# Parking the gating results in DRAM and re-spacing five stages of a one-core decoder step

## The chip, the cores and the metric

The kernel runs on one core of one Trainium2 chip. The metric is the device time of one execution in microseconds (us). Three runs of the kernel before took 2204.79, 2202.24 and 2200.46 us, so its median is 2202.24 us. Its engines are named PE (TensorE), DVE (VectorE), ACT (ScalarE), POOL (GpSimd) and SP (SyncE, which issues nearly all DMAs).

## The reference

One layer of a decoder trunk over 1024 prompt tokens and 32 sample tokens (8 requests of 4), with model width 1024. Reduced to what the kernel's stages compute:

```python
h = layer_norm(ALPHA * x + 0.5 * swiglu(x, f1_w1, f1_w3, f1_w2))      # FFN A, LN1
z = h @ w_in + b_in                                                   # q, k, v | u, v | gates ga, gb
# attention: 3 groups of 4 heads, (window, dilation) = (128,1), (512,4), (2048,16), T5 bias
att = sum over groups of o_g * softmax_g(logsumexp_g)                 # combine_groups
# spatial gating
z = gelu(uv); u, vr = z[..., :512], z[..., 512:]
vn = layer_norm(vr, ln_g, ln_b)
yb = u * (tril(ws) @ vn + sb)                                         # in chunks of 128 tokens, 4 groups of 128
mix = (sigmoid(ga) * (att @ w_oa) + sigmoid(gb) * (yb @ w_ob)) @ w_out
h = layer_norm(ALPHA * h + mix)                                       # LN2
h = layer_norm(ALPHA * h + 0.5 * swiglu(h, f2_w1, f2_w3, f2_w2))      # FFN B, LN3
```

where `swiglu(x, w1, w3, w2) = (silu(x @ w1) * (x @ w3)) @ w2` with a hidden width of 2816.

## The kernel before, in words

Activations lie transposed: features on the 128 partitions, the 1056 tokens as columns, in four chunks `c` of 264. Every float32 operand of a product is split into a rounded half `hi` and a remainder `lo` (`split`: a cast on ACT, a subtraction on DVE), and a product is three matmuls, hi x hi, hi x lo and lo x hi (`mm3`, L227). All weights come in units of 128 x 1024 or smaller (`unit`: a load into a raw tile, then a split).

In order of time, the stages are: FFN A's hidden blocks by a Strassen scheme (to about 467 us); the down product w2, most of it in nine rounds of seven products (467 to 657), then four plain blocks in dense form, one output block after the other, their evictions at L885; LN1, chunk by chunk (`start_ln`, `norm`); six gate blocks; the other products of z in pairs; ten more gate blocks ("tail gates", to about 1240) beside which the attention and the spatial gating run; w_ob; w_oa; w_out with LN2; FFN B in the same way as A; LN3.

The work beside the products is written as generators. After each product block, `tick` lets the queues `bg`, `slow` and `mid` make a few steps each, so the attention (`attend`, six times: two pairs of heads by three groups), the gating (`sgu_norm`, then four `sgu_mix`) and the norms come between products. One attention step computes scores (L1164), a masked minimum on DVE (L1172), exponentials on ACT (L1176), transposes on PE (L1187) copied back by L1191, and the products with the values (L1203). After each attention its maxima and sums (`ml`) are transposed (L1225) and stored to the DRAM tensor `mlD`; after three attentions a combine reads them back, computes the softmax over the groups (L1261 to L1274), stores the factors to `cD` (L1276) and loads them spread over the partitions (L1283), by which the attention outputs are multiplied (L1288 to L1291). The scheduler orders instructions on each engine by recorded order and priority; `high_priority` and `urgent` move something ahead, `issue_after` holds something behind.

Lines that the later steps touch: `sgu_norm` normalises v over tokens, with a square root on ACT (`rsqrt`, L630) and nine normalisations (L1447). `sgu_mix` writes its split result into two tiles `yb[gg]` that stay in SBUF until w_ob. `mix` multiplies each product of w_ob or w_oa into its gate (L1505). `units2` makes the w2 units for the dense blocks, of which the last come while the dense blocks run. `column_sums`, `centers` subtract the column means for LN1 (L537). `copy_state` appends state copies `ws<-st`, which no one waits for, to weight loads. The pool of 128 x 1056 tiles has 37 slots (`S`), that of weight halves 8 (`W`).

Of the kernel before, what the change touches and what calls it, by code (L numbers as in the profile page):

```python
# [13 lines left out]
F32R = mybir.dt.float32r  # L14
AF = mybir.ActivationFunctionType
# [5 lines left out]
P = 128  # L21
# [39 lines left out]
LATE = 16  # L61
# [3 lines left out]
WARM = 2  # L65
FENCED = (mybir.EngineType.DVE, mybir.EngineType.Activation, mybir.EngineType.SP)
# [5 lines left out]
EARLY = 6  # L72
# [7 lines left out]
class Trunk:  # L80
# [131 lines left out]
    def unit(self, src, n=D, slot=False, ahead=URGENT):  # L212
        new = self.S if slot else self.W
        with self.tc.high_priority(offset=ahead):
            raw = self.R([P, D])
# [3 lines left out]
        self.fence[mybir.EngineType.SP] = dma.ins  # L219
        self.copy_state(dma, 1)  # L220
        return hi, lo
# [133 lines left out]
    def prep(self, src, f, H, engine):  # L355
# [7 lines left out]
        self.copy_state(dma, 2)  # L363
# [154 lines left out]
    def center(self, c, hs, rest, m=None, parts=1):  # L518
# [15 lines left out]
        for j in range(2):  # L534
# [3 lines left out]
            yield  # L538
# [43 lines left out]
    def norm(self, c, i, mode, Y, s):  # L582
# [7 lines left out]
        r, t = self.X([P, 3], "rs"), self.X([P, 3], "rt")  # L590
        self.rsqrt(r, t, pv, EPL)
# [35 lines left out]

    def rsqrt(self, r, t, v, eps):
# [12 lines left out]
    def ffn(self, w13, w2p, w2, i, mode, resid):  # L641
        nc, preps = self.nc, {}
        last = FB + NG * (KB // 2) - 1
# [27 lines left out]
        else:  # L671
# [3 lines left out]
            self.step(self.bg, 1)  # L675
            begin(1)
            for c in range(NC):
                self.drain(lns.pop(c))
                self.hidden8(units, 0, c)
                if c:  # L680
                    with self.chained():
                        next(preps[1], None)
            self.bg.append(s1)
# [5 lines left out]
        def ready(f):  # L689
            for _ in preps.pop(f):  # L690
                pass
            if f < last:
                begin(f + 1)

        def between(f, bg, slow=0):
            if f + 1 in preps:
                next(preps[f + 1], None)
# [8 lines left out]
        for f in range(1, FB):  # L706
# [5 lines left out]
            def after():  # L712
# [4 lines left out]
            self.hidden(f, after)  # L717
# [67 lines left out]
    def out(self, w2, i, mode, ready, between, load):  # L785
        nc = self.nc
        f = FB
        self.w2units, self.spare = self.units2(w2), False
# [4 lines left out]
        def fetch(k):  # L793

            if k < NPL:
                H.append(self.load_hidden(k))

# [33 lines left out]
        for g in range(NG):  # L831
            for np in range(KB // 2):
                final = g == NG - 1 and np == KB // 2 - 1
                if g == NG - 2 and np == 0:
                    self.bg.append(sums)
                if g == 0 and np == 1 and mode != "out":
# [7 lines left out]
                ready(f)  # L844

                def step(p):
# [6 lines left out]
                    if final:  # L853
                        fetch(k + 1)
                        if k in (4, 6):
                            W2.append(next(self.w2units))
# [16 lines left out]
        self.spare = True  # L873
# [13 lines left out]
        for c in range(NC):  # L887
            early = 6 if c == 0 else 0
            if mode != "out":
                self.hold_normed(c)  # L890
                if c == 2:
                    self.early = [self.unit(self.a["wzp"][n], slot=True, ahead=AFTER) for n in range(CHUNKED)]
            for n in range(KB):
# [4 lines left out]
                if c == 0 and n in (1, 3):  # L898
                    W2.append(next(self.w2units))
# [147 lines left out]
    def widen(self):  # L1047
# [6 lines left out]
        self.jD = self.dp.tile([6, 64, 66], F32, name="jD")  # L1054
        self.zD = [self.dp.tile([P, NT], F32, name=f"zD{n}") for n in range(42)]
# [21 lines left out]
        for n in range(CHUNKED, NLEAD):  # L1077
            w = self.unit(a["wzp"][n])
            if n == NLEAD - 1:
                begin(0)  # L1080
            for c in (1, 3, 0, 2):
                self.gate8(w, DENSE[n], c, AF.Sigmoid, STEPS["lead"], 1)
                if n == NLEAD - 1:
                    next(preps[0], None)
# [33 lines left out]
    def attend(self, i):  # L1118
# [19 lines left out]
        self.fetch_qkv(i + 1)  # L1138
# [77 lines left out]
        for t in range(6):  # L1216
# [4 lines left out]
            if t < 4:  # L1221
                scores(t)
            yield from self.pause(SPREAD)
# [12 lines left out]
    def combine(self, hp):  # L1236
# [3 lines left out]
        for g in range(3):  # L1240
            x = raw[:, g]
            for m in range(2):
                for h in range(2):
                    src = self.mlD[hp, g, m, h]
                    o = x[8 * h : 8 * h + 8, m]
                    if g == 0:
                        nc.sync.dma_start(o, src.rearrange("(a x) -> a x", a=8))
                    elif g == 1:
                        nc.sync.dma_start(
                            o.rearrange("p (r b) -> p r b", r=4), src.rearrange("(r a b) -> a r b", r=4, a=8)  # L1250
# [543 lines left out]
```

## Time and profile before

| What | Value |
|---|---|
| Median of three runs | 2202.24 us (2200.46 to 2204.79) |
| The profiled execution | 2200.98 us |
| Its span | 2199.2 us |
| Mean granted TensorE clock | 0.988 |
| Instructions | 43234 |
| PE, DVE, ACT, POOL busy | 97%, 71%, 41%, 15% |
| DMA moved | 429.82 MB, mean 195 GB/s |

The profile gives one execution. Its time is 1.8 us longer than its span, since the span begins with the first instruction recorded. In a row of a group, "x" gives the number of instructions, then come busy time and mean ns of one, then the idle time of that engine just before them and the operation that ended most of it. "A <- B" in a row of waits reads: A waited for B. A granted clock of 1.00 is full speed.

### The profile page before, as it was taken

The numbers are of one execution on the slowest core, as the hardware profiler recorded it, in microseconds if no ns is written. First come the engines' busy times: TensorE is split into PE (matmuls) and PEld (weight loads), VectorE is DVE, ScalarE is ACT, GpSimd is POOL, SyncE is SP. The second block draws the span as 40 slices with busy tenths as digits, with TensorE's granted clock in tenths as the row PEclk, the third lists the DMA queues.
The fourth block names the chain that finished last, engine by engine and source line by source line (L and its number), as shares of the span: only waits on it lengthen the run. The fifth ranks groups of instructions, "written<-read, shape, count | busy, mean of one in ns | idle before, by whom it ended". The sixth has DMA issues, their size and how long they took to land.

```text
span 2199.2 us, 43234 instructions
## 1 busy us (share of the span) xinstructions
PE 2133.2 (97%) x17281; PEld 2092.9 (95%) x17281; DVE 1564.8 (71%) x2718; ACT 898.1 (41%) x1690; POOL 330.1 (15%) x238
## 2 busy tenths in 40 slices
PE   9999999999998999999989998998999999999997
PEld 8999999999998999999879897998999999999997
DVE  8777776656788725887674648778676776657787
ACT  5444444421225634344465354246444444322224
POOL 0432332200010022232000000000432332100000
PEclk9999999999999999999989999999999999999999
DMA  4435545598873325666854547513445545596751
GB/s 157 146 134 177 179 161 177 193 367 324 330 279 136 135 102 188 215 215 221 313 165 152 172 156 245 187 51 126 165 158 178 171 161 185 186 384 264 295 192 79
DMA packets 170553, 429.82 MB, mean 195 GB/s; under 512 B 24864, under 2 KB 61456, under 8 KB 167664
## 3 DMA queue, kind: packets, MB, share of 16 engines
q1 hardware_dynamic: 169920, 426.53, 55.3%
q8 instruction: 135, 2.21, 0.4%
q10 hardware_dynamic: 432, 0.54, 0.1%
q14 instruction: 66, 0.54, 0.1%
HBM read 305.97 MB, written 167.22 MB: 215 GB/s over the span
## 4 chain that ended last, share of the span: by engine, by line
PE 81%; DMA 7%; DVE 7%; ACT 2%; issue 1%; POOL 1%; SPq 1%; ACTq 0%; DVEq 0%; POOLq 0%
PE ax L227 43%; PE mm L227 35%; DMA M<-kv 4%; DVE W L239 1%; PE ax L1164 1%; DMA zD<-M 1%; DMA S<-zD 1%; PE ax L1203 1%; DVE S L239 1%; PE ax L1187 1%; DMA R<-wz 0%; DVE X L1346 0%; DVE S L608 0%; DVE X L1361 0%; DVE M L1345 0%
## 5 line engine op out<-in xcount | busy, mean ns | idle before, releaser
L227 PE MATMUL ax<-S,W 128*128 128x264 f32 x5472 | 716.2, 284 | 0.8 <-ACT S L994 0.5
L227 PE MATMUL mm<-S,W 128*128 128x264 f32 x5040 | 677.4, 289 | 25.8 <-DVE S L1505 9.3
L227 PEld LDWEIGHTS ax<-S,W 128*128 128x128 f32 x5472 | 685.6, 188 | 3.3 <-ACT S L994 1.5
L227 PEld LDWEIGHTS mm<-S,W 128*128 128x128 f32 x5040 | 641.6, 191 | 43.1 <-issue 10.7
L227 PE MATMUL ax<-S,S 128*128 128x264 f32 x3288 | 483.7, 285 | 2.9 <-DVE S L1003 2.8
L227 PEld LDWEIGHTS ax<-S,S 128*128 128x128 f32 x3288 | 434.2, 188 | 4.1 <-DVE S L1003 4.1
L227 PE MATMUL mm<-S,S 128*128 128x264 f32 x2496 | 388.4, 286 | 9.0 <-ACT S L238 4.0
L227 PEld LDWEIGHTS mm<-S,S 128*128 128x128 f32 x2496 | 337.7, 189 | 11.5 <-ACT S L238 4.4
L238 ACT CAST W<-R 128x256 fp32r<-128x256 f32 (+2 forms) x172 | 127.6, 759 | 316.8 <-PE mm L227 118.2
L369 POOL TENSOR_TENSOR Q<-R 128x512 f32<-128x512 f32 x50 | 72.1, 1443 | 793.1 <-DMA R<-w13b 217.1
L239 DVE TENSOR_TENSOR W<-R,W 128x256 fp32r<-128x256 f32 (+2 forms) x172 | 152.6, 891 | 28.2 <-ACT W L238 24.0
L238 ACT CAST W<-Q 128x1024 fp32r<-128x1024 f32 (+1 forms) x79 | 77.9, 986 | 217.1 <-POOL Q L370 91.7
L780 DVE SCALAR_TENSOR_TENSOR S<-ax,S 128x264 f32<-128x264 f32 x240 | 99.9, 431 | 69.6 <-PE ax L227 68.5
L444 DVE TENSOR_TENSOR S<-ax,M 128x264 f32<-128x264 f32 x84 | 33.7, 433 | 150.6 <-PE ax L227 150.6
L106 POOL CAST S<-ones 128x1 fp32r<-128x1 f32 x32 | 18.3, 594 | 745.5 <-PE mm L227 663.8
L239 DVE TENSOR_TENSOR S<-Q,S 128x1024 fp32r<-128x1024 f32 (+1 forms) x79 | 111.8, 1415 | 3.5 <-ACT S L238 3.3
L239 DVE TENSOR_TENSOR W<-Q,W 128x1024 fp32r<-128x1024 f32 (+1 forms) x79 | 92.0, 1164 | 24.5 <-ACT W L238 24.5
L238 ACT CAST S<-Q 128x1024 fp32r<-128x1024 f32 (+1 forms) x79 | 77.8, 985 | 74.1 <-PE ax L227 55.0
L238 ACT CAST S<-R 128x512 fp32r<-128x512 f32 (+1 forms) x65 | 44.6, 686 | 116.5 <-DMA sumsA<-S 42.6
L239 DVE TENSOR_TENSOR S<-S,M 128x528 fp32r<-128x528 f32 x72 | 85.6, 1189 | 2.1 <-ACT M L238 0.2
L370 POOL TENSOR_TENSOR Q<-Q,R 128x512 f32<-128x512 f32 x50 | 83.6, 1673 | 2.7
L377 POOL TENSOR_TENSOR Q<-R,Q 128x512 f32<-128x512 f32 x50 | 82.7, 1653 | 1.2
(199 smaller groups left out, 2063.3 us busy)
## 6 DMA issues: line engine op xcount, KB each, us to landing
ws<-st SPq DMA_DIRECT2D x144, 256.0 KB
S<-sumsA SPq DMA_DIRECT2D x63, 528.0 KB
S<-sumsB SPq DMA_DIRECT2D x63, 528.0 KB
M<-kv SPq DMA_DIRECT2D x96, 256.0 KB
sumsA<-M SPq DMA_DIRECT2D x90, 264.0 KB
sumsB<-M SPq DMA_DIRECT2D x90, 264.0 KB
R<-w13b SPq DMA_DIRECT2D x44, 512.0 KB
S<-zD SPq DMA_DIRECT2D x42, 528.0 KB
```

Of the source, the lines that this page charges most:

```text
L106: self.nc.gpsimd.tensor_copy(t[:, 0, :1] if len(shape) == 3 else t[:, :1], self.ones[:, :1])
L227: mm = lambda a, b, s, e: nc.tensor.matmul(o, a[:, cc], b, start=s, stop=e, skip_group_check=True)
L238: a = self.nc.scalar.copy(hi, src)
L239: b = self.nc.vector.tensor_tensor(lo, src, hi.bitcast(F32), op=ALU.subtract)
L369: tt(s12[:, lo], cd[:, lo], cd[:, hi], op=ALU.add)
L370: tt(s12[:, hi], s12[:, lo], ab[:, lo], op=ALU.subtract)
L377: tt(s34[:, hi], ab[:, hi], s12[:, hi], op=ALU.subtract)
L444: go(one, 5, False, lambda x: tt(h[:, x, 1], one[x], p7[:, x], op=ALU.add))
L780: nc.vector.scalar_tensor_tensor(y(x, r, e), bank[x], HALF, y(x, r, e), op0=ALU.mult, op1=ALU.add)
L1164: nc.tensor.matmul(pS[h][:, r, :nk], q[e, i * P : (i + 1) * P], k[e, k0 : k0 + nk], start=True, stop=True)
L1187: nc.tensor.transpose(pT[r][:, h, o], s[:, r, h, o], self.ident)
L1203: nc.tensor.matmul(pv[0][e, (i % 4) * P : (i % 4 + 1) * P], V[:, i - (nb - 1) + b, e], sT[:, r, h, b * P : b * P + P], start=b == 0, stop= ...
```

## The change

All parts are in one file:

- **Gate weights ahead.** `part_gates` loads the six lead gate units while FFN A's seven-product rounds run, splits them, and stores both halves to DRAM (`gates`). `gate_unit` loads the halves, so no split remains at the gate blocks. The rounds carry one state copy fewer for each pair of weight loads, and `units2` none.
- **w2 units.** All four are made in the last seven-product round (`last`, `FINAL`), the centre subtractions of a chunk are spaced.
- **Norms.** `rsqrt_dve` computes an inverse square root on DVE, by an integer estimate and three Newton steps. It replaces the square root on ACT in the last chunk of LN2, in chunk 2 of LN3, and in `sgu_norm`. After LN2's chunk 2, ACT evaluates a Silu once.
- **FFN B's first blocks.** Blocks 0 and 19 are computed densely at the start, where before block 0 alone was; 19 was in the Strassen scheme.
- **Spatial gating.** Its steps are spaced, the sample rows of v are written out by a generator of their own (`sgu_rows`) at the end, and each `sgu_mix` stores its two halves to DRAM (`ybD`); `fetch_yb` loads them in four places during the last tail gates (`load`, `FETCH`), the fourth result after them.
- **Attention loads.** The next attention's q, k, v are loaded at step 3 of the running one instead of its beginning; a combine reads `mlD` in nine loads instead of twelve and loads the factors of its third group later.
- **w_ob.** `EARLY` goes from 6 to 5: blocks 5, 6 and 7 are computed at w_oa's blocks 1, 3 and 5, instead of blocks 6 and 7 at w_oa's blocks 0 and 1. Sigmoids of late gates change place with it, and `LATE` goes from 16 to 6.

The core of the diff:

```diff
+    def part_gates(self, *units):
+        yield from self.pause(4 * MID)
+        for n in units:
+            lo, hi = self.S([P, D]), self.S([P, D], F32R)
+            self.nc.sync.dma_start(lo, self.a["wzp"][n])
+            yield from self.pause(2 * MID)
+            self.split(hi, lo.bitcast(F32R), lo)
+            yield from self.pause(MID)
+            for t, dst in zip((hi.bitcast(F32), lo), self.gates[n]):
+                self.nc.sync.dma_start(dst, t)
+            yield
...
+    def rsqrt_dve(self, r, t, x, v, eps):
+        nc = self.nc
+        tt = nc.vector.scalar_tensor_tensor
+        nc.vector.tensor_scalar(x, v, eps, None, op0=ALU.add)
+        nc.vector.tensor_scalar(r.bitcast(I32), x.bitcast(I32), -0.5, MAGIC, op0=ALU.mult, op1=ALU.add)
+        for _ in range(3):
+            nc.vector.tensor_tensor(t, x, r, op=ALU.mult)
+            tt(t, t, -0.5, r, op0=ALU.mult, op1=ALU.mult)
+            self.chain = tt(r, t, 1.5, r, op0=ALU.add, op1=ALU.mult).ins
...
+            lead = [units] + [[self.unit(w13[f, x]) for x in range(2)] for f in plain[1:]]
             begin(1)
             for c in range(NC):
                 self.drain(lns.pop(c))
-                self.hidden8(units, 0, c)
...
+                for f, u in zip(plain, lead):
+                    self.hidden8(u, f, c)
...
-            yield self.unit(w2[u * n : u * n + n].rearrange("(p x) -> p x", p=P), D, self.spare)
+            yield self.unit(w2[u * n : u * n + n].rearrange("(p x) -> p x", p=P), D, u > 1, raw=self.Q if u > 1 else self.R, copies=0)
...
-                if c == 0 and n in (1, 3):
-                    W2.append(next(self.w2units))
...
-        self.rsqrt(rs[:, 0], rs[:, 1], mv[:, :, 1], EPS)
+        self.rsqrt_dve(rs[:, 0], rs[:, 1], mv[:, :, 1], mv[:, :, 1], EPS)
...
+        yield from self.pause(MID)
+        for t, dst in zip((hi, lo), self.ybD[gg]):
+            nc.sync.dma_start(dst, t.bitcast(F32))
+
+    def fetch_yb(self, gg):
+        t = [self.S([P, NT], F32R) for _ in range(2)]
+        for x, src in zip(t, self.ybD[gg]):
+            self.nc.sync.dma_start(x.bitcast(F32), src)
+        self.yb[gg] = t
...
+        def load(c):
+            while any(g in self.mid for g in sgu[: c + 1]):
+                self.step(self.mid, 1)
+            with self.tc.high_priority(offset=URGENT):
+                for g in FETCH[c][1]:
+                    self.fetch_yb(g)
+                for n in FETCH[c][0]:
+                    mt[n] = self.fetch_z(34 + n)
...
-            if n < KB - EARLY:
-                local(EARLY + n)
+            if n % 2 and EARLY + n // 2 < KB:
+                local(EARLY + n // 2)
```

with `FETCH = ((), ((0,), (0,)), ((1, 2), (1,)), ((3,), (2,)), ((4, 5), (3,)))`: for each chunk, the gates and then the gating results to load; the last entry is for the call after the tail gates.

The order that the scheduler makes of it, at three places. First SP, at the second combine, before: the loads from `mlD` have gone ahead, the factors are stored and spread, and gate loads (`zD`) follow.

```order
L1276 DMA cD<-S_15282 16x128 x3
L1283 DMA S_15315<-cD 64x1024 x2
L1283 DMA S_15316<-cD 64x1024 x2
L1283 DMA S_15317<-cD 64x1024
L1102 DMA S_15434<-zD_8671 128x1056
L1102 DMA S_15511<-zD_8672 128x1056
```

And now, at the same place:

```order
L1289 DMA mlD<-X_15271 32x128
L1304 DMA S_15318<-mlD 16x2x128
L1309 DMA S_15318<-mlD 8x4x32 x4
L1626 DMA Q_15823<-wout 128x1024
L1309 DMA S_15318<-mlD 8x16x8 x4
L1333 DMA cD<-S_15318 16x128 x3
L1343 DMA S_15348<-cD 64x1024 x2
L1343 DMA S_15351<-cD 64x1024 x2
L1343 DMA S_15388<-cD 64x1024
L1562 DMA S_15460<-yb_8666 128x1056
L1562 DMA S_15461<-yb_8667 128x1056
L1160 DMA S_15464<-zD_8706 128x1056
```

The two halves of the fourth gating result (`yb_8666`, `yb_8667`) now stand behind the combine's loads.

Second PE, at the end of the last attention. Before, w_ob products (a tile of w_ob is `W_15583` or `W_15584`, a gating result `S_13534` to `S_13919`) run beside it and go on after the ml transpose (L1225).

```order
L1187 MATMUL ax_15189<-ident,S_15135 128x128 x2
L1187 MATMUL ax_15188<-ident,S_15135 128x128 x2
L1225 MATMUL ax_15235<-ident,X_14981 32x128
L227 MATMUL mm_15631<-S_13765,W_15583 128x264
L227 MATMUL mm_15631<-S_13766,W_15583 128x264
L227 MATMUL mm_15631<-S_13765,W_15584 128x264
L227 MATMUL mm_15631<-S_13918,W_15583 128x264
```

Now, with the third result in `S_15279` and `S_15280` and the fourth in `S_15460` and `S_15461` (products of the same form in between are left out):

```order
L1285 MATMUL ax_15269<-ident,X_15011 32x128
L1261 MATMUL ax_15217<-S_15228,Q_14998 64x128 x4
L253 MATMUL mm_15477<-S_15279,W_15469 128x264
...
L253 MATMUL mm_15517<-S_15280,W_15469 128x264
L253 MATMUL mm_15517<-S_15279,W_15470 128x264
L253 MATMUL mm_15477<-S_15460,W_15469 128x264
```

After the ml transpose (now L1285) come four value products and nine products with the third result, and then products with the fourth. Three tiles (`mm_15477`, `mm_15495`, `mm_15517`) are begun in parallel, since the first three results are used ahead of the fourth.

Third ACT, at the gating's norm. Before:

```order
L630 ACT_TABLE_LOAD
L630 ACTIVATE X_13274<-X_12957,eps_163 128x9
L1145 COPY Q_13366<-ax_13367 128x512
L1210 COPY S_12932<-ax_13231 128x512
L1145 COPY Q_13366<-ax_13373 128x512
L1447 ACTIVATE S_12952<-S_12952,X_13274 128x512 x2
L1447 ACTIVATE S_12953<-S_12953,X_13274 128x512 x2
L1447 ACTIVATE S_12954<-S_12954,X_13274 128x512 x2
L1447 ACTIVATE S_12955<-S_12955,X_13274 128x512 x2
L1447 ACTIVATE S_12956<-S_12956,X_13274 32x512
L1176 ACT_TABLE_LOAD
L1176 ACTIVATE S_13415,X_13413<-S_13415,X_13413 128x128
```

Now (L1009 evicts a gate product, L1234 are the exponentials, L1249 copies transposes):

```order
L1249 COPY S_13447<-ax_13440 128x512
L1249 COPY S_13447<-ax_13439 128x2x128
L1511 ACTIVATE S_12976<-S_12976,X_13468 128x512 x2
L1511 ACTIVATE S_12977<-S_12977,X_13468 128x512 x2
L1511 ACTIVATE S_12978<-S_12978,X_13468 128x512 x2
L1511 ACTIVATE S_12979<-S_12979,X_13468 128x512 x2
L1511 ACTIVATE S_12980<-S_12980,X_13468 32x512
L1009 ACTIVATE M_13714<-mm_13689,cols 128x264
L1234 ACTIVATE S_13450,X_13422<-S_13450,X_13422 128x128
```

The square root and both table loads have gone; the nine normalisations still follow each other.

More of the change, by code (lines that the diff above doesn't have):

```diff
@@ L60 @@
 AFTER = 100
-LATE = 16
+LATE = 6
 MID = 3
@@ L642, in ffn @@
         nc, preps = self.nc, {}
-        last = FB + NG * (KB // 2) - 1
+        plain = PLAIN[: 1 if i == 0 else 2]
+        blocks = [f for f in range(FB) if f not in plain] + [FB + g for g in range(NG * (KB // 2))]
+        after = dict(zip(blocks, blocks[1:]))
         def begin(f):
@@ L704, in load @@
                     loads.popleft()()
-        for f in range(1, FB):
+        for f in blocks[: FB - len(plain)]:
             ready(f)
@@ L1536, in mix @@
         units = self.A = None
-        while any(g in self.mid for g in sgu):
-            self.step(self.mid, 1)
+        load(NC)
         def column_sums():
```

158 lines of the change are left out of this document (98 added, 60 removed).

## The prediction

> **What bounds the kernel now.** I read the page first, then the waits of TensorE by stretch, then the stretches with the largest loss. The page: TensorE is busy nearly all the time and holds four fifths of the chain that ended last.
>
> ```profile
> span 2199.2 us, 43234 instructions
> PE 2133.2 (97%) x17281; PEld 2092.9 (95%) x17281; DVE 1564.8 (71%) x2718; ACT 898.1 (41%) x1690; POOL 330.1 (15%) x238
> PE 81%; DMA 7%; DVE 7%; ACT 2%; issue 1%; POOL 1%; SPq 1%; ACTq 0%; DVEq 0%; POOLq 0%
> ```
>
> The stretches (from:to, length, busy time with number of instructions for PE, weight loads, DVE, ACT, POOL, then granted clock, DMA share, GB/s) give the price of a product and show where TensorE loses.
>
> ```profile
> 50.00:460.00 410.00, 410.00 (x3367) 410.00 (x3366) 293.30 (x400) 175.71 (x311) 121.58 (x76) 1.00 0.51 174
> 1080.00:1345.00 265.00, 244.61 (x1990) 220.60 (x1991) 158.31 (x463) 137.62 (x367) 0.00 (x0) 0.96 0.58 183
> 1120.00:1160.00 40.00, 30.96 (x223) 26.37 (x223) 32.41 (x85) 25.13 (x60) 0.00 (x0) 0.79 0.61 187
> 460.00:660.00 200.00, 199.57 (x1604) 194.92 (x1603) 145.82 (x316) 39.72 (x63) 5.99 (x12) 1.00 0.86 324
> 1342.00:1388.00 46.00, 38.28 (x268) 35.86 (x269) 42.27 (x67) 21.40 (x25) 1.93 (x2) 0.93 0.67 232
> 1480.00:1530.00 50.00, 43.24 (x331) 42.09 (x331) 44.58 (x56) 32.27 (x45) 3.28 (x4) 0.93 0.37 128
> ```
>
> Undisturbed, 410 us hold 3367 products: 0.122 us each. That is TensorE's pace, and a change that leaves the products alone can win only where it idles or is granted a lower clock. The attention stretch 1080:1345 idles for 20.4 us at a clock of 0.96. The waits of TensorE (who waited for whom: us, times, longest) name the causes, in turn for 1060:1400, 655:710 and 1480:1540:
>
> ```profile
> PE ax L1187 <- ACT S L1176: 10.0, 4, 5.9
> PE mm L227 <- DVE S L1505: 9.3, 9, 3.2
> PE mm L227 <- ACT M L954: 5.0, 3, 2.9
> PE mm L227 <- ACT S L238: 2.3, 1, 2.3
> ```
>
> ```profile
> PE mm L227 <- DVE S L885: 3.8, 3, 2.5
> PE mm L227 <- DVE S L239: 2.4, 1, 2.4
> ```
>
> ```profile
> PE mm L227 <- ACT S L238: 4.0, 1, 4.0
> PE mm L227 <- ACT M L415: 2.7, 3, 1.9
> ```
>
> **What the change wins.** *w2 and LN1.* Before, four unit splits of w2 stand in VectorE's queue among the evictions of the dense w2 blocks (L885), next to unbroken centre subtractions.
>
> ```profile
> 672.62 1.22 DVE L239 TENSOR_TENSOR S<-R,S 128x1024 fp32r<-128x1024 f32 x1
> 673.75 2.42 DVE L537 TENSOR_TENSOR S<-S,ax 128x1056 f32<-128x1056 f32 x2
> ```
>
> The change makes all four units in the last seven-product block and spaces the subtractions, so 4 x 1.22 = 4.9 us of VectorE leave this place. The 3.8 + 2.4 = 6.2 us of waits lose their cause: I take -6 (range -7 to -2, if the last loads of that block land late).
>
> *Gating norm.* ScalarE held its queue for a square root with its table load, nine normalisations, and the load back before the attention's exponentials could run:
>
> ```profile
> 1119.93 1.28 ACT L630 ACT_TABLE_LOAD   x1
> ...
> 1124.34 6.46 ACT L1447 ACTIVATE S<-S,X 128x512 f32<-128x512 f32 x9 [0.27 <-DVE X L1443]
> 1130.82 1.28 ACT L1176 ACT_TABLE_LOAD   x1
> ```
>
> Both table loads go (2.56 us). The nine normalisations still stand in one run, but the changed order puts 16 + 59 = 75 products between the scores and transposes on either side of it, 75 x 0.122 = 9.1 us, against 6.46 us and four exponentials. The stretch 1120:1160 shows 9.0 us without TensorE, and its clock of 0.79 costs 31 x 0.21 = 6.5 us more; of these 15.5 I take -12 (-15 to -5). Of the other waits for exponentials (10.0 - 5.9 = 4.1) and of the 5.0 for gate outputs the slower pace of the gating should remove half: -5 (-8 to +2). The new rsqrt is some eleven tiny VectorE instructions in series; the trace has none, so I bound it between 0 and 11 x 0.42 = 4.6 (the row of L1505 below, a far larger operation) and cost it at nothing, because gate products go on beside it.
>
> *w_oa stage.* Here VectorE is the bound: in 1342:1388 it is busy 42.3 of 46 us, while 268 products need 32.7. Two more w_ob blocks come into this stretch. Each brings 48 x 0.122 = 5.9 us of TensorE work, but only four product evictions and a weight split to VectorE (groups of 1312:1322.6: busy, mean ns):
>
> ```profile
> L1505 DVE TENSOR_TENSOR S<-S,mm 128x264 f32<-128x264 f32 x7 | 2.9, 416 | 3.4 <-PE mm L227 3.4
> ...
> L239 DVE TENSOR_TENSOR W<-R,W 128x512 fp32r<-128x512 f32 x1 | 0.7, 671 | 0.0
> ```
>
> 4 x 0.42 + 0.7 = 2.4 us. So 11.7 us of products are done for 4.8 us of VectorE, a win of 6.9 if the interleaving is perfect and 0 if it is not at all: -6 (-8 to -1). Two table loads more (the late gates' sigmoids and the sample softmax now alternate) lie on ScalarE, busy 21.4 of the 46 us.
>
> *FFN B's start.* The 4.0 + 2.7 us of waits go with the table switches around the last LN2 chunk:
>
> ```profile
> 1497.79 1.28 ACT L630 ACT_TABLE_LOAD   x1
> ...
> 1499.37 1.28 ACT L415 ACT_TABLE_LOAD   x1
> ```
>
> With the second plain block some 140 products stand between the last chunk's norm and its first use, where 24 stood. Doing it densely costs 24 products, 2.9 us; the clock (0.93 over 43 us) gives back some 3. Sum -5 (-7 to +1).
>
> The Trainium skill, ScalarE: Activation LUTs, section "What ACT_TABLE_LOAD costs", puts a switch at about 2.66 us, because a drain follows the load. By the rows a switch is 1.28 us; by that page the switches removed here (four of them on the path) would be worth 5.5 us more than their rows, an estimate from the page.
>
> **What the change costs.** Parking the gating results moves 8.5 MB through DRAM. What matters is where the last reload stands. In the changed SyncE order it comes behind the whole second combine: ml to DRAM, nine loads back, VectorE's combine, three stores to cD, five broadcast loads, and only then the two halves of result 3. TensorE's order has the first w_ob products behind attention 5, each needing result 3 for its last quarter; the 27 products of three tiles that do without it are used up earlier. The trace of before shows that same chain, harmless there because the results never left SBUF:
>
> ```profile
> 1309.29 0.27 PE L1225 MATMUL ax<-ident,X 128*32 128x128 f32 x1
> ...
> 1322.60 1.26 SPq L1276 DMA_DIRECT2D cD<-S  x3
> 1324.02 3.04 SPq L1283 DMA_DIRECT2D S<-cD  x5
> ...
> 1329.24 1.23 DVE L1288 TENSOR_TENSOR S<-S,S 128x1024 f32<-128x1024 f32 x1 [1.61 <-DMA S<-cD]
> ```
>
> From the ml transpose to the end of the five issues are 1327.1 - 1309.3 = 17.8 us. Twelve loads become nine (-1 us), and VectorE is not shared with the seven product evictions of the row above (-2.9 us): 14. Then the reload must land: the first broadcast load took 1329.2 - 1324.0 = 5.2 us; the reload (1.08 MB behind 1.3 MB of broadcast data) I put at 7 (5 to 13). That is 21 us after the transpose. Cover: value products and nine w_ob products, some 2 us. So TensorE waits **+19** (+8 if ScalarE and VectorE run ahead, +25), and after such an idle time the clock dips: +2, from 1120:1160, where 0.21 over 10 us is 2.1.
>
> The Trainium skill, TensorE: Matmul & The Clock Gate, Part 1, says that after an idle window of some 3.4 us the clock falls to half and needs as long of work to return; by that, one wait of 19 us costs 1.7 us of clock, an estimate from the page, no more than one of 6 us. The row above, 6.5 us lost over several waits, agrees in kind.
>
> Attention 5 now runs with 18 products beside it, where it had 149 in 1287:1312 (groups of TensorE, then of ScalarE):
>
> ```profile
> L227 PE MATMUL mm<-S,W 128*128 128x264 f32 x149 | 20.2, 289 | 0.0
> ```
>
> ```profile
> L1176 ACT ACTIVATE S<-S,X 128x128 f32<-128x128 f32 x16 | 6.2, 391 | 1.1 <-DVE X L1172 1.1
> L1176 ACT ACTIVATION_READ_ACCUMULATOR S<-S,X 128x1 f32 x16 | 3.0, 187 | 0.0
> L1191 ACT COPY S<-ax 128x256 f32<-128x256 f32 x8 | 2.6, 375 | 9.0 <-PE ax L1187 9.0
> ```
>
> A step on ScalarE is (6.2 + 3.0 + 2.6) / 4 = 3.0 us. Ahead of it stand transposes and the first masked score, for which I add 0.9 (0 to 2): four steps are 15.6 us. TensorE's own work there is 25 - 149 x 0.122 = 6.8 us and 18 products, 2.2: 9.0. So **+7** (+4 to +11). But the 131 products are not lost: they follow the wait, where they cover the end of the combine. So the 3.2 us for L1505 and the 2.3 for L238 at 1336 to 1343 go: -5 (-5.5 to 0).
>
> *DMA elsewhere.* The gates' halves and fewer state copies add some 6 MB to the seven-product stage, whose DMA share is 0.86: 28 us are free there, and 6 MB at 324 GB/s need 19. State copies of about 2 MB move to the program's start. Both beside TensorE work: +2 (0 to +8).
>
> **The sum.** -6 - 12 - 5 - 6 - 5 - 5 = -39; +19 + 2 + 7 + 2 = +30; together -9. The profiled execution took 2200.98 us (its span and 1.8 us around it), 1.3 less than the median of 2202.24. 2200.98 - 9 = **2192 us**.
>
> **Rivals.** *The reload is slower than I think, and the kernel ends slower.* Behind the reload stand four z loads of 0.54 MB, issued at once. If they share the engines with it, 1.08 + 2.16 MB at the 232 GB/s of 1342:1388 take 14 us in place of 7; with attention 5 at its upper end (+4), the clock twice as long low (+2) and two more of the gating gains lost: 2192 + 7 + 4 + 2 + 2 = **2207**. It decides from a wait of about 30 us. For it: small and broadcast transfers stand ahead in one queue. Against: the reload is issued first.
>
> *The wait is hidden.* If attention 4 and 5 end late for TensorE anyway, or the combine is quick, result 3 is there: 2192 - 19 - 2 = **2171**. Against it: the chain is in series and has nothing to overlap but 2 us.
>
> *The change does not do what it says.* VectorE is at 32.4 of 40 us in 1120:1160; spacing its work may only move the waits to the next attention step and to the w_oa stage. Then the -12, -5 and -6 halve: 2192 + 11 = **2203**.
>
> **How the numbers follow.** Forecast 0.50, slow reload 0.26, hidden wait 0.14, no effect 0.10. By the terms' bounds the forecast alone reaches from 2182 to 2201; of it 0.39 lies over 0.2% (4.4 us, about what a measurement tells from no change) below 2202.24, 0.10 within. Faster 0.39 + 0.14 = 0.53; same 0.10 + 0.07 = 0.17; slower 0.30. The range takes most of the hidden wait and of the slow reload: 2172 to 2212.
>
> **What would show it.** Right: in the changed trace one wait of TensorE of 15 to 25 us just ahead of the w_ob products, released by the load of the parked result, and no wait over 3 us at the gating norm, at w2's dense blocks and at FFN B's start. Wrong: that wait is under 8 us; or 1080:1345 keeps its old waits; or seven-product loads hold TensorE.

## The result and the profile after

The changed kernel takes 2215.19 us (median of 6 runs, 2214.74 to 2218.43). The kernel before took 2202.16 us (median of 6 runs, 2200.46 to 2205.56). The ratio is 1.0054, with a 95% interval of 1.0044 to 1.0064: 13 us slower, beyond the end of the range, where 10 us faster was forecast. The profiled execution after took 2218.43 us, the longest of the six, so its span lies 17.2 us over that of before.

The page after, first its head, then the chain's shares, then the group in which TensorE idles most:

```profile
span 2216.4 us, 43347 instructions
PE 2134.5 (96%) x17305; PEld 2093.8 (94%) x17305; DVE 1559.8 (70%) x2731; ACT 892.2 (40%) x1680; POOL 315.3 (14%) x234
PE 81%; DMA 10%; DVE 5%; ACT 2%; issue 1%; SPq 1%; POOL 0%; ACTq 0%; DVEq 0%; POOLq 0%
...
L253 PE MATMUL mm<-S,W 128*128 128x264 f32 x5208 | 696.8, 288 | 39.0 <-DMA S<-yb 25.5
```

TensorE's busy time is that of before (2133.2). What was added is idle time, and it changed hands in the chain: DMA went from 7% to 10%, VectorE from 7% to 5%. Of the 39.0 us that the dense products were held, 25.5 go to loads of the parked results. The stretches, columns as before:

```profile
460.00:660.00 200.00, 193.38 (x1525) 187.23 (x1524) 147.58 (x309) 45.43 (x69) 4.00 (x5) 0.99 0.90 337
1080.00:1345.00 265.00, 220.23 (x1775) 196.42 (x1776) 146.59 (x437) 133.92 (x360) 0.00 (x0) 0.91 0.63 206
1120.00:1160.00 40.00, 39.15 (x341) 35.46 (x339) 29.54 (x86) 26.50 (x68) 0.00 (x0) 1.00 0.48 147
...
1342.00:1388.00 46.00, 42.52 (x340) 41.55 (x339) 35.19 (x77) 15.31 (x22) 0.00 (x0) 1.00 0.52 168
1480.00:1530.00 50.00, 48.63 (x400) 48.21 (x399) 43.47 (x70) 29.57 (x50) 3.62 (x6) 1.00 0.34 114
```

Three places got better: the gating norm (1120:1160 holds 341 products and transposes where 223 stood), the w_oa stage (340 for 268) and FFN B's start (400 for 331). Two got worse. The attention stretch as a whole idles 44.8 us in place of 20.4, at a clock of 0.91 in place of 0.96, and the seven-product stage (460:660), which had idled 0.4 us, idles 6.6. TensorE's waits in 1060:1400:

```profile
PE mm L253 <- DMA S<-yb: 25.5, 4, 20.4
PE ax L1202 <- DMA S<-zD: 7.4, 4, 3.5
PE ax L1245 <- ACT S L1234: 6.0, 6, 2.1
PE mm L253 <- DVE S L1582: 4.3, 5, 1.3
...
PE mm L253 <- ACT M L1009: 2.9, 1, 2.9
```

Two kinds of loads stand on top: parked results (`yb`), for which the trace of before has no wait, and attention inputs (`zD`, stored parts of z), which there held TensorE once in this window, for 1.3 us. The waits of before for VectorE's gating of w_ob products (L1505, now L1582) fell from 9.3 to 4.3 us.

The timeline shows the longest one as a chain on SyncE's queue (SPq) and TensorE, from the maxima's store to the first product that was held:

```profile
1305.22 0.32 SPq L1289 DMA_DIRECT2D mlD<-X  x1
...
1316.56 1.24 SPq L1333 DMA_DIRECT2D cD<-S  x3
1317.90 3.04 SPq L1343 DMA_DIRECT2D S<-cD  x5
1320.98 1.06 SPq L1562 DMA_DIRECT2D S<-yb  x2
...
1327.58 1.03 PE L253 MATMUL mm<-S,W 128*128 128x264 f32 x3 [20.35 <-DMA S<-yb]
```

The reload is issued 15.8 us after the maxima go out, and lands 6.6 us later; TensorE stands 20.35 us. The last two attentions look like this on TensorE (in brackets the idle time just before a row, and what ended it):

```profile
1271.85 0.88 PE L1261 MATMUL ax<-S,Q 128*64 128x128 f32 x12 [2.62 <-ACT S L1249]
1275.86 1.03 PE L253 MATMUL mm<-S,W 128*128 128x264 f32 x3 [3.13 <-DMA S<-yb]
1284.62 1.94 PE L1202 MATMUL ax<-ident,S 128*128 128x128 f32 x8 [3.50 <-DMA S<-zD]
1289.78 0.66 PE L1245 MATMUL ax<-ident,S 128*128 128x128 f32 x4 [2.07 <-ACT S L1234]
1293.15 1.11 PE L1245 MATMUL ax<-ident,S 128*128 128x128 f32 x4 [1.13 <-ACT S L1234]
1296.80 1.03 PE L253 MATMUL mm<-S,W 128*128 128x264 f32 x3 [1.38 <-DMA S<-yb]
1304.12 0.66 PE L1245 MATMUL ax<-ident,S 128*128 128x128 f32 x4 [1.48 <-ACT S L1234]
```

With a last one of 0.41 us these are 15.7 us: 8.0 behind loads (3.13, 3.50, 1.38), 7.7 behind ScalarE. The first two, 5.7 us, stand at the end of attention 4, the other 10.0 in attention 5. The clock in these stretches, by two windows of 20 us:

```profile
1260.00:1280.00 20.00, 14.24 (x108) 12.99 (x109) 8.62 (x24) 7.88 (x20) 0.00 (x0) 0.85 0.74 211
1280.00:1300.00 20.00, 11.93 (x76) 9.11 (x73) 7.61 (x28) 9.64 (x32) 0.00 (x0) 0.67 0.92 317
```

Busy time times one less the clock, summed over windows of 1 us from 1240 to 1340, gives 11.4 us lost (before 1.5). It is not the long wait that costs most of them: 8.8 are lost before 1300, and 2.0 behind that wait, from 1327.5 on, as these two windows show:

```profile
1325.00:1330.00 5.00, 1.76 (x6) 1.45 (x7) 3.35 (x3) 0.00 (x0) 0.00 (x0) 0.50 1.01 377
1330.00:1335.00 5.00, 5.00 (x35) 5.00 (x34) 2.99 (x8) 1.59 (x2) 0.00 (x0) 0.79 1.03 344
```

### The profile page after: what moved, and what is told of

Same layout as the page of the kernel before. It is cut to its first block, busy times and chain, and to the rows that moved or that the text cites. A ratio compares the mean times of both kernels' runs of the same rounds, so it can differ in the third digit from the quotient of the medians.

```text
span 2216.4 us, 43347 instructions
## 1 busy us (share of the span) xinstructions
PE 2134.5 (96%) x17305; PEld 2093.8 (94%) x17305; DVE 1559.8 (70%) x2731; ACT 892.2 (40%) x1680; POOL 315.3 (14%) x234
## 4 chain that ended last, share of the span: by engine, by line
PE 81%; DMA 10%; DVE 5%; ACT 2%; issue 1%; SPq 1%; POOL 0%; ACTq 0%; DVEq 0%; POOLq 0%
PE ax L253 43%; PE mm L253 36%; DMA M<-kv 2%; DMA S<-zD 1%; DMA R<-w2pa 1%; DMA S<-partA 1%; DVE W L265 1%; DMA zD<-M 1%; DMA S<-yb 1%; PE ax L1222 1%; DMA S<-sumsA 1%; DVE S L265 0%; DVE X L1425 0%; PE ax L1261 0%; DMA R<-wz 0%
## 5 line engine op out<-in xcount | busy, mean ns | idle before, releaser
L253 PE MATMUL mm<-S,W 128*128 128x264 f32 x5208 | 696.8, 288 | 39.0 <-DMA S<-yb 25.5
L253 PEld LDWEIGHTS mm<-S,W 128*128 128x128 f32 x5208 | 659.2, 190 | 55.9 <-DMA S<-yb 26.6
L253 PEld LDWEIGHTS ax<-S,W 128*128 128x128 f32 x5400 | 678.4, 188 | 10.7 <-ACT W L264 3.9
L253 PE MATMUL ax<-S,S 128*128 128x264 f32 x3240 | 476.9, 284 | 3.5 <-DVE S L1058 3.3
L253 PEld LDWEIGHTS ax<-S,S 128*128 128x128 f32 x3240 | 427.6, 188 | 5.1 <-DVE S L1058 4.8
L264 ACT CAST W<-R 128x1024 fp32r<-128x1024 f32 (+3 forms) x170 | 125.8, 756 | 294.7 <-PE mm L253 130.6
L395 POOL TENSOR_TENSOR Q<-R 128x512 f32<-128x512 f32 x49 | 66.3, 1352 | 800.3 <-DMA R<-w13a 182.0
L265 DVE TENSOR_TENSOR W<-R,W 128x1024 fp32r<-128x1024 f32 (+3 forms) x170 | 145.5, 858 | 35.5 <-ACT W L264 35.0
L265 DVE TENSOR_TENSOR S<-Q,S 128x1024 fp32r<-128x1024 f32 (+1 forms) x82 | 119.9, 1462 | 4.6 <-ACT S L264 4.6
L401 POOL TENSOR_TENSOR Q<-R,R 128x512 f32<-128x512 f32 x49 | 73.1, 1493 | 18.4 <-ACT M L466 18.4
```

Of the source, the lines that this page charges most:

```text
L253: mm = lambda a, b, s, e: nc.tensor.matmul(o, a[:, cc], b, start=s, stop=e, skip_group_check=True)
L264: a = self.nc.scalar.copy(hi, src)
L265: b = self.nc.vector.tensor_tensor(lo, src, hi.bitcast(F32), op=ALU.subtract)
L395: tt(s12[:, lo], cd[:, lo], cd[:, hi], op=ALU.add)
L401: tt(s34[:, lo], ab[:, lo], cd[:, lo], op=ALU.subtract)
```

## The experiments

Beside the ratios I use one length, called "the stretch": in one profiled execution, from the first transposes of values (L1144 before at 1074.5, L1202 after at 1076.2) to the product with ones for the first centre subtraction of w_out (1420.8 and 1442.9). It is 346.3 us before, 366.7 after. The first theory was that the reload behind the combine, with what it starves of cover, is the whole loss. The rivals: the seven-product stage, the later attention loads, or parking as such. A median of before is from the same chip as the kernel beside it; on these chips it took 2203.48 to 2206.05 us, up to 3.9 more than in the runs above. Ratios allow for that, lengths of single executions do not (0.6 us for the stretch, if it is spread evenly).

**Results kept in SBUF (e1).** The change without parking.

```diff
-        for t, dst in zip((hi, lo), self.ybD[gg]):
-            nc.sync.dma_start(dst, t.bitcast(F32))
+        self.yb[gg] = (hi, lo)
...
-                for g in FETCH[c][1]:
-                    self.fetch_yb(g)
```

> The gating results stay in SBUF, as before; all other parts of the change stay. The theory of the parked results: the wait of 20.4 us for the last reload, the smaller ones of 3.1, 1.4 and 0.7 us for the other reloads, some 10 us of lowered clock around them, and the idle time of an uncovered last attention all go, because w_ob products run beside it again: 2215 - 35 = about 2180 us. The rival, that the later loads and the spaced gating lose the time and the reload only shows it: TensorE waits as long for something else in the same stretch, above 2205 us.

Measured: 2199.27 us against 2203.48, ratio 0.9985 (0.9974 to 0.9997). The stretch is 354.2 us, in a profiled execution that was the longest of the ten (2205.26). TensorE's waits in 1060:1440:

```profile
PE mm L253 <- DVE S L1579: 14.5, 8, 8.3
PE ax L1245 <- ACT S L1234: 9.6, 4, 4.2
```

All waits for parked results are gone, and with them the loss. But what takes their place costs too: 8.3 us now stand at the combine's end (1330), where the w_ob products that the reload had held back are used up by then, and 4.2 + 3.2 us at 1151 and 1158, where the gating norm's win had been.

**The last reload ahead of the combine (e2).** Parking stays; the fourth result is loaded with the third.

```diff
-FETCH = ((), ((0,), (0,)), ((1, 2), (1,)), ((3,), (2,)), ((4, 5), (3,)))
+FETCH = ((), ((0,), (0,)), ((1, 2), (1,)), ((3,), (2, 3)), ((4, 5), ()))
...
-            while any(g in self.mid for g in sgu[: c + 1]):
+            while any(g in self.mid for g in sgu[: c + 1 + (c == NC - 1)]):
```

> Result 3 is reloaded together with result 2, ahead of the second combine; nothing else differs. The theory that the reload's place behind the combine is the cause: the wait of 20.4 us falls under 3 us and the clock dip after it goes (some 4 us), while the last attention stays uncovered: 2215 - 22 = about 2193 us. The rival, that TensorE has nothing to do there whatever the order (parking as such is the cause): the wait goes to the combine or to the attention, above 2208 us.

Measured: 2198.01 us against 2203.48, ratio 0.9975 (0.9964 to 0.9986). The stretch is 346.5 us. Waits in 1060:1440:

```profile
PE mm L253 <- DVE S L1582: 7.9, 9, 1.5
PE ax L1245 <- ACT S L1234: 5.6, 5, 2.1
PE ax L1202 <- DMA S<-zD: 5.0, 2, 3.4
...
PE mm L253 <- DMA S<-yb: 2.0, 1, 2.0
```

Two lines, and the kernel is faster than before: (1.0054 - 0.9975) x 2203.5 = 17.4 us for the place of two loads in a queue. The short waits at the last attentions stay (2.62, 2.04, 3.44, 2.07 and three shorter ones, 13.1 us for 15.7), and so does the clock: by the same reckoning 10.2 us are lost in 1240:1340 without the long wait, for 11.4 with it. So the 20 us were the difference between winning and losing.

**No gate halves (e3).** The six lead gate units are loaded and split as before.

```diff
-                if g < NG - 1 and np == 0 and mode != "out":
-                    self.mid.append(self.part_gates(*range(g, NLEAD, NG - 1)))
...
-            w = self.gate_unit(n)
+            w = self.unit(a["wzp"][n])
```

> The lead gates' weights are loaded and split at their blocks, as before, and no halves are parked; all else stays. If the parked halves cost the 9 us that the seven-product stage of FFN A lost: 2215 - 9 = 2206 us, with up to 6 us given back where the splits return to the gate blocks (2206 to 2212). If the loss in that stage comes from the w2 units made in its last block: 2215 us.

Measured: 2216.55 us against 2203.48, ratio 1.0061 (1.0042 to 1.0080), no difference from the change that can be measured. The seven-product stage ends 6.5 us sooner (660.1 for 666.6), but from there to the first sample rows of z it takes 154.1 us for 150.5: the splits come back at the gate blocks. The longest wait left in 460:666 is for the attention's bias tables, which the change makes sooner there (`LATE` 6 for 16):

```profile
PE ax L997 <- DVE M L993: 2.7, 1, 2.7
```

**No state copies in the seven-product stage (e4).**

```diff
-        self.copy_state(dma, 2 if n == D else 1)
+        self.copy_state(dma, 3 if n == D else 0)
```

> The state copies leave the seven-product stage altogether (11 fewer there, 6 MB) and go beside the Strassen blocks. If that stage lost its 9 us to the amount of DMA: 2215 - 7 = 2208 us or better. If it lost them to the order in which loads and splits stand (weights behind gate halves): no change, 2213 to 2216 us.

Measured: 2221.07 us against 2203.48, ratio 1.0082 (1.0067 to 1.0097), slower than the change. The longest of TensorE's waits in 460:666:

```profile
PE mm L253 <- DMA S<-sumsA: 8.6, 3, 8.1
```

Less to move (319 GB/s in 460:660 for 337), and a longer wait, behind sums whose loads SyncE issues after five spread loads of the bias tables (4.79 us of issuing at 517.2). So the amount alone does not set the time of this stage. Why exactly these loads landed late was not separated.

**The reload ahead, no gate halves, bias tables as before (e5).** e2 and e3 together, and:

```diff
-LATE = 6
+LATE = 16
```

> The reload of result 3 ahead of the combine, no parked gate halves, and the bias tables as late as before (LATE 16). The theory that the seven-product stage lost its 9 us to the gate halves and the early tables: its end comes back to within 1 us of before, and against the kernel with the reload ahead alone (about 0.9975 of before) some 5 us less: ratio 0.995, about 2192 us. The rival, that what the stage wins the gate blocks pay back in splits: ratio 0.997 to 0.998, about 2197 us.

Measured: 2194.76 us against 2205.77, ratio 0.9949 (0.9933 to 0.9965). It beats both kernels. The stretch of the last two attentions:

```profile
1240.00:1340.00 100.00, 81.15 (x616) 72.06 (x615) 55.39 (x158) 42.11 (x108) 0.00 (x0) 0.88 0.71 228
```

And the largest of its waits in 1060:1440:

```profile
PE ax L1200 <- DMA S<-zD: 8.4, 3, 3.8
```

The seven-product stage ends at 655.0 (before 657.6), with no wait of TensorE; the stretch is 345.0 us. The next 155.6 us to the sample rows are 0.9 less than before, where the change with its gate halves took 6.0 less: of the -6 put down to w2 and LN1, 3.6 to 5.1 came from the gate halves (154.1 in e3, 155.6 here, 150.5 with them), and the seven-product stage pays more for them, 6.5, than they bring.

**The change without its costs (e7).** SBUF as in e1, no gate halves and `LATE` 16 as in e5, attention loads at the beginning, and:

```diff
-EARLY = 5
+EARLY = 6
```

with w_ob's blocks at w_oa's 0 and 1. What is left is w2's units, the norms, FFN B's start, the gating's spacing, the combine's fewer loads and the moved state copies.

> Only the parts that won in the trace of the change: w2 units in the last round, norms with the inverse square root on VectorE, two dense first blocks in FFN B, the spaced gating. Gating results stay in SBUF; attention loads, tables, EARLY and the lead gates are as before. If the gains add up: 2202 - 6 - 5 - 12 = about 2180 us. The rival, that products as cover are a fixed amount, so that what the gating no longer waits for returns as a wait at a later attention step or at the last combine: the gating's 12 us are given back in good part, 2188 to 2193 us.

Measured: 2195.52 us against 2205.77, ratio 0.9955 (0.9937 to 0.9973), no different from e5. The stretch is 349.7 us, and waits in 1060:1440 are as large as ever:

```profile
PE mm L253 <- DVE S L1575: 18.3, 8, 10.8
PE ax L1243 <- ACT S L1232: 11.7, 4, 4.4
```

**The gating alone (e8).** The kernel before with `rsqrt_dve` in `sgu_norm`, its spacing and `sgu_rows`, nothing else.

```diff
-            yield
+            yield from self.pause(2)
...
-        self.rsqrt(rs[:, 0], rs[:, 1], mv[:, :, 1], EPS)
+        self.rsqrt_dve(rs[:, 0], rs[:, 1], mv[:, :, 1], mv[:, :, 1], EPS)
```

> The kernel before with the spaced gating and its inverse square root on VectorE alone. If the 15 us lost around the gating's norm (9.0 us idle and 6.5 of clock) are won for the whole kernel: about 2190 us. If cover is a fixed amount and the waits move to later steps of the attention: 2198 to 2203 us.

Measured: 2198.22 us against 2205.77, ratio 0.9967 (0.9953 to 0.9981): 4 to 10 us won. The stretch of the profiled execution is 346.4 us, as long as before. The largest of its waits in 1060:1440:

```profile
PE ax L1199 <- ACT S L1188: 10.6, 4, 4.3
```

The wait of 5.9 us is gone, yet the exponentials hold TensorE as long in sum as before (10.0): 4.3 and 1.1 us at 1145 and 1150, 3.8 at 1256. So the ratio shows a win, but it cannot be found in the stretch where it was made.

**All reloads early (e9).** The change with `FETCH` so that all four results are asked for before the last two tail chunks:

```diff
+FETCH = ((), ((0,), (0, 1, 2)), ((1, 2), (3,)), ((3,), ()), ((4, 5), ()))
```

> The change with all four parked results reloaded before the last attention (one or two chunks of gates earlier), all else as changed. If the last attention's bare run costs what the trace shows, some 8 us of idle time and 6 to 8 of lowered clock, of which half is covered now: against the kernel with result 3 alone ahead (0.9975 of before) 6 us less, ratio 0.995, about 2191 us. If the earlier loads meet waits for free tiles or the combine loses its cover instead: ratio 0.997 to 0.999.

Measured: 2206.81 us against 2205.77, ratio 1.0001 (0.9991 to 1.0012); stretch 354.7 us. Waits in 1060:1440:

```profile
PE mm L253 <- DVE S L1582: 9.6, 5, 6.0
PE mm L253 <- DMA S<-yb: 8.4, 2, 7.1
PE ax L1202 <- DMA S<-zD: 7.6, 2, 6.0
```

Earlier is not better without limit: the loads now bunch, and a reload and an attention's inputs each hold TensorE 6 to 7 us.

**Attention loads as before (e10).** e5 with the next attention's loads at the beginning of the running one:

```diff
-        follower = i + 1
+        self.fetch_qkv(i + 1)
```

> As the kernel with the reload ahead and without gate halves (e5, ratio 0.9949), but each attention's q, k, v are loaded at the beginning of the one ahead, as before the change. If the later loads cost the waits that the trace shows for them (3.8, 2.5 and 2.1 us): 6 us less than e5, ratio 0.992. If the loads take their tiles from the reloads instead, or the waits move to the next step of the attention: 0.994 to 0.998.

Measured: 2196.71 us against 2206.05, ratio 0.9957 (0.9942 to 0.9972), e5's within the intervals. Waits in 1060:1440:

```profile
PE ax L1243 <- ACT S L1232: 10.2, 4, 5.3
PE mm L253 <- DMA S<-yb: 7.0, 1, 7.0
...
PE ax L1200 <- DMA S<-zD: 2.6, 1, 2.6
```

The waits for inputs go from 8.4 to 2.6 us, those for a reload and for exponentials grow by 2.7 and 5.1. The later loads are not the loss.

**Parking alone (e12).** The kernel before, only `sgu_mix` storing to DRAM and `fetch_yb` at the change's places.

```diff
-        self.yb[gg] = (hi, lo)
...
+        for t, dst in zip((hi, lo), self.ybD[gg]):
+            nc.sync.dma_start(dst, t.bitcast(F32))
```

> The kernel before with the gating results parked in DRAM and reloaded as in the change, and nothing else of it. If the parking is what loses the time: a wait of about 20 us for the last reload, a bare last attention, less the 5 us at the end of the combine: about 2220 to 2228 us. If it only loses in company with the spaced gating and the later loads: 2200 to 2206 us.

Measured: 2215.25 us against 2206.05, ratio 1.0048 (1.0032 to 1.0064); stretch 362.6 us. The longest wait in 1060:1440:

```profile
PE mm L228 <- DMA S<-yb: 19.9, 3, 18.3
```

Parking alone, with the reloads at these places, makes the loss; all other parts of the change together, put on top of it, move nothing that can be measured (1.0054).

**Four steps a product block (e16, e17).** The queues beside the tail gates are advanced faster, to end the attentions while products are left. e16 is the change with this line; e17 keeps results in SBUF, without gate halves and with `LATE` 16.

```diff
-STEPS = dict(lead=6, strassen=3, seven=2, out=2, tail=3, wob=2, wout=3)
+STEPS = dict(lead=6, strassen=3, seven=2, out=2, tail=4, wob=2, wout=3)
```

> The change with one number other: four steps of the attention for each gate chunk in place of three, so the attention runs further ahead and gate products are left for the last attention; the reloads stay behind the second combine. If a bare last attention costs about 15 us (8 us idle, the rest a clock of 0.67 to 0.85) apart from the reload: the wait for the reloads stays near 20 us or grows, the last attention is covered, 2215 - 13 = about 2202 us. If both are one wait that has to come somewhere: 2213 to 2217 us.

> Results in SBUF, lead gates and tables as before, four attention steps for each gate chunk; spaced gating, w2 units, norms, FFN B's first blocks, later attention loads and the w_ob interleaving of the change. If cover is what decides (gate products beside the last attention, 240 w_ob products beside the combine): the stretch from the first attention to w_out falls under 336 us, about 2185 us. If the uncovered steps only move (attention 2 stands bare in this order): 2193 to 2198 us.

Measured: e16 2226.8 us against 2206.05, ratio 1.0094 (1.0070 to 1.0118), stretch 377.2 us; e17 2195.26 us, ratio 0.9956 (0.9939 to 0.9972), stretch 348.5 us. Waits in 1060:1440 of e16, then of e17:

```profile
PE mm L253 <- DMA S<-yb: 47.9, 8, 23.5
```

```profile
PE mm L253 <- DVE S L1577: 16.9, 10, 10.7
PE ax L1243 <- ACT S L1232: 12.8, 5, 7.2
```

In e16 the attentions end sooner and two reloads hold TensorE, 19.0 us at 1303 and 23.5 at 1329. In e17 the attention at 1159 stands bare in place of the last (7.2, 3.1 and 1.9 us), and the combine still holds 10.7 us.

**What they show together.** The loss is the place of the last reload: moved ahead of the combine (e2) it is gone, and parking with that place, put alone into the kernel before (e12), makes it. And no version's stretch is under 345.0 us, whichever wait it removes. A product can stand beside only one thing. The gating norm's 15 us, the combine's 5 and the last attention's 10 are covered out of the same stock, and what covers one uncovers another. That is an argument from the lengths of single executions, and no run adds or takes away products to test it; the ratios of e5, e7, e10 and e17, 0.9949 to 0.9957, agree with it, but do not tell these versions apart. Nor is it shown that no order gets under 345 us. Of the times named ahead of the runs, both theories missed in e1, e4, e9, e12 and e16.

## Why the prediction was wrong

Its terms against the two traces (us; measured is idle time and clock at the term's place):

| Term | Predicted | Measured |
|---|---|---|
| w2 and LN1 | -6 | -6.0, from the end of the seven products to the sample rows (156.5 to 150.5) |
| Gating norm | -12 | -14.7 in 1120:1160 (8.2 of idle time, 6.5 of clock) |
| Other attention and gate waits | -5 | +0.6 (idle 7.6 to 6.6 in 1076.2:1120 and 1160:1264, 1.6 of clock more) |
| w_oa | -6 | -4.2, from 1345 to w_out (idle 6.9 to 4.8, clock 2.1 to 0) |
| FFN B's start | -5 | -5.0, from w_out to the end of FFN B (713.5 to 708.5) |
| End of the combine | -5 | -5.4 (waits of 3.18 and 2.26 gone) |
| Wait for the last reload | +19 | +21.0 (20.35 + 0.66) |
| Clock after it | +2 | +9.9 in 1240:1340 (1.5 to 11.4) |
| Last attention bare | +7 | +15.7, with the end of the one before it |
| DMA elsewhere | +2 | +9.0, in the seven-product stage |

The measured terms come to +20.9. The pairs of z, for which there was no term, took 1.3 us less, and idle time and clock together grew by 2.4 us more than the length of the stretch did; that rest, of times that are modelled, is not resolved. So 17.2. The bounds were drawn too tight as well: the terms, each at its bound, add up to 2164 at the one end and 2242 at the other, not to the 2182 and 2201 that the forecast gives for them.

**Right: the mechanism of the long wait.** The wait stands where it was announced, for the named reload, behind the named chain, 23.0 us after the transpose of the maxima (1304.61), where 21 was summed. The places of the wins were right too. At the gating the table loads went, and the new root takes 2.2 us on VectorE, inside its bounds: eleven instructions from 1130.65 to 1132.86, of which this is the first:

```profile
1130.65 0.17 DVE L663 TENSOR_SCALAR X<-X 128x9 f32<-128x9 f32 x1
```

The rule of the Trainium skill that would have made the table loads worth more does not hold here. Before, the normalisations ended at 1130.80, the load started at 1130.82, and ScalarE's next exponential started 1.30 us after it:

```profile
1132.12 0.40 ACT L1176 ACTIVATE S<-S,X 128x128 f32<-128x128 f32 x1
```

That leaves no room for the 2.66 us in the Trainium skill, ScalarE: Activation LUTs, section "What ACT_TABLE_LOAD costs".

**The step that failed is the price of the bare attention: "+7" for attention 5 and "+2" for the clock.** In attention 5 TensorE idled 10.0 us, inside the term's bounds, but only 5.1 of them behind ScalarE, from whose rows the 7 were worked out; 4.9 were behind loads (3.50 and 1.38), which came for nothing in that sum. The end of attention 4 had no term at all, and there TensorE stood 5.7 us, 2.62 behind ScalarE and 3.13 behind a reload. The change asks for these loads late, between other reloads and spread factors in one queue, and the DMA share was 0.92 in 1280:1300. The clock was taken from one wait, and for that one the 2 were right: 2.0 us are lost behind it. But the clock was low where TensorE worked in pieces, 0.67 in 1280:1300 with TensorE at work 60% of the time, and 8.8 us were lost from 1240 to 1300, ahead of that wait. By the Trainium skill, TensorE: Matmul & The Clock Gate, Part 1, the one wait was to cost 1.7 us, an estimate, and the 2.0 behind it agree. The same part describes, under HAM oscillation, a loop in which every wait is longer than a window of some 3.4 us; here all the waits from 1238 to 1300 but one (3.50) were shorter, and the clock fell all the same. Together the two terms missed 8.7 + 7.9 us. The run e2 fits this: without the long wait, the prediction's own sum came to 2171, and e2, at 0.9975 of before, lies some 26 us over it, so the miss is not in the reload's term.

**The second is "+2" for the DMA elsewhere**, 7.0 us short. The engines did have a free share, which went from 0.86 to 0.90 busy, and the stage took 9.0 us longer even so: e3 and e5 give 6.5 us back by leaving out the gate halves and 5.1 by the bias tables' later place. TensorE's largest waits there are for split weights (3.5 us in all, behind ScalarE), and ScalarE's longest wait for a load of w2 is 18.1 us, where it was 11.4. The halves' own gain was booked under w2, so that term was right in size by luck and wrong in cause.

**The third is "-5" for the other waits**, 5.6 us short. Those for gate outputs fell from 5.0 to 2.9 us, but an attention's inputs held TensorE 1.91 us at 1239, where they had not, and 1.6 us went to the clock after two waits at the first attention (1.53 and 2.94 us), which had stood before too (1.30 and 2.93) and had cost no clock.

The other terms missed by 2.0 (reload), 1.8 (w_oa), -0.4 and -2.7 (gating). With 16.6, 7.0 and 5.6, less the 1.3 and 2.4 above, these are the 26 us between -9 and +17.2.

**The rivals and the signs.** The slow reload named the right side at the wrong price: the reload took 6.6 us, not 14, and a wait of 20 us decided, below the 30 that it asked for. The hidden wait fell with the 20.35. "Does not do what it says" holds in part, and in a way that was not priced: each win is there at its place, and in e1, e7 and e8 waits come up further on in its stead. Every sign that was to show the forecast right came, the one wait of 15 to 25 us and no wait over 3 us at the gating norm, w2's dense blocks and FFN B's start. Of the signs against it, the one about the seven-product stage came in part: TensorE idled 6.6 us there, though only 0.6 of them directly behind loads. The signs of being right tested terms that the sum had, and the loss was where it had too little or none.

## What to carry to other kernels

A result parked in DRAM cost here what stood ahead of its reload in the issuing queue, 15.8 us, more than the 6.6 us of the reload itself: look up what that queue waits for, and put the reload ahead of any chain that goes out and comes back. Count the products that are free as cover once, and book each against one wait only; in these runs a wait removed by spending them showed up where they were. And when a stretch is left bare, price its input loads and the clock over the whole stretch, not only the slowest engine in it.

## What the hardware showed

The clock fell without a long wait. Three windows of 5 us around 1270:

```profile
1265.00:1270.00 5.00, 4.22 (x35) 4.01 (x33) 1.35 (x4) 1.86 (x4) 0.00 (x0) 1.00 0.47 143
1270.00:1275.00 5.00, 0.88 (x12) 0.64 (x12) 2.82 (x10) 3.54 (x12) 0.00 (x0) 0.91 1.00 263
1275.00:1280.00 5.00, 4.14 (x20) 3.85 (x22) 0.28 (x1) 0.96 (x2) 0.00 (x0) 0.50 1.05 304
```

Over two waits of 2.62 and 3.13 us, with 0.88 us of work between them, the granted clock went from 1.00 to 0.50. At 0.50 eight transposes (L1202 at 1284.62) took 1.94 us, where eight at 1124.37, at 1.00, had taken 1.04.

The length of the waits does not settle it. At the first attention the two kernels have nearly the same two waits, 1.30 and 2.93 us before, 1.53 and 2.94 after, and this is the window in which the second one ends, before and then after:

```profile
1080.00:1085.00 5.00, 3.98 (x33) 3.98 (x34) 4.90 (x10) 2.40 (x5) 0.00 (x0) 1.00 0.99 336
```

```profile
1080.00:1085.00 5.00, 2.32 (x11) 2.32 (x12) 4.19 (x7) 2.27 (x5) 0.00 (x0) 0.80 0.96 316
```

Likewise one wait of 1.91 us (until 1238.98, after) was followed by a clock of 0.66 in 1240:1245, while one of 2.77 us (until 1252.38, before) left it at 1.00 to 1260. What decides it is not shown.

Open stay the reason why fewer state copies made the seven-product stage slower (e4), by which of its loads the gate halves hold that stage, and what sets the clock at waits as short as these.
